# Loading the first pair of a batched matrix product in half-height pieces

## The chip, the cores and the metric

The kernel runs on one core of a Trainium2 chip. The metric is the device time of one execution in microseconds. TensorE (PE in the profile) multiplies matrices, VectorE (DVE) here converts float32 to bfloat16, ScalarE (ACT) copies results out of PSUM, SyncE (SP) issues all the transfers, and GpSimd (POOL) only waits at the end. The transfers themselves run on 16 DMA engines. On-chip memory (SBUF) has 128 partitions; a tile's first dimension is its partitions.

## What is computed

```
batch, m, k, n = 16, 512, 512, 512
a: (batch, k, m) float32     b: (batch, k, n) float32
out = matmul(a.transpose(0, 2, 1), b)      # (batch, m, n) float32
```

Each of the 16 batches is a 512x512x512 product in which both operands have k as their rows. 33.55 MB are read and 16.78 MB written.

## The kernel before

The 16 batches go in 8 pairs. One transfer brings both batches of a pair for one operand, 2 MB, into a tile `x` of 128 partitions: 64 partitions for each batch (`G = 2`, `Q = 64`), and in each partition 8 consecutive rows of k (`R = 8`), which is 16 KB in one run. So partition q of a batch holds k = 8q to 8q + 7. Four such tiles, x0 to x3, are used in turn: transfer n loads operand a for even n and b for odd n, of pair n // 2, into tile n % 4.

SyncE's program is written out by hand (lines 65 to 71). It issues the 16 loads in order. The first four have no wait; from n = 4 on (line 67) it waits on `s_in`, which VectorE raises when it has read a tile for the last time (lines 84 to 88, a one-element memset named `done`). After the loads come the stores of the first seven pairs, each waiting on `s_out` (line 70), all on the same queue. The last store is issued at line 133 after everything else.

VectorE (lines 73 to 88) converts each tile in two halves of 4 rows per partition (`V = 2`, `RV = 4`): first half v = 0 of a and b, then v = 1 of a and b. The wait on the loads stands at line 81, once per tile; the conversion is line 82. The v = 0 conversions of the next pair wait until TensorE has read the v = 0 buffers (`s_v`, line 76), those of v = 1 until the pair's products are finished (`s_mm`, line 78).

TensorE runs a loop of 8 pairs (line 92). For each it does 64 products of 64 rows of k by 128 by 512, 32 for each v, and the two batches of a pair use the upper and lower 64 rows of its array in turn (line 103). A sum over k is spread over v, r and 64 partitions; the order in which k is laid out doesn't matter so long as a and b have the same. ScalarE copies the sums to one of seven output tiles `o` (line 121) and signals the store (line 126).

## Time and profile before

| what | value |
|---|---|
| median of 3 runs | 124.03 us (123.98 to 124.14) |
| profiled execution: its own time | 123.82 us |
| profiled execution: span | 121.9 us |
| bytes moved | 50.33 MB, 413 GB/s over the span |
| DMA engines busy | 97.6% |
| PE / DVE / ACT busy | 51% / 31% / 26% |
| transfers | 8 of a, 8 of b, 8 of out, 2048 KB each |

The span is the time from the first to the last instruction in one profiled execution; the execution's own time is 1.9 us more. In the profile "L68" is line 68 of the kernel, an arrow "x<-in_a_dram" means that tile x is written from in_a_dram, "xN" counts instructions, and "A <- B" in a list of waits means that A waited for B (total us, times, longest). "SPq" is SyncE's own program. The DMA share is the mean busy share of the 16 DMA engines.

### The profile page before, as it was taken

The page shows a single profiled execution, that of the slowest core. Times are in us where ns is not written, and L with a number is a line of the kernel's source. Part 1 is how long each engine was busy: PE and PEld are TensorE (multiplying, and loading weights), DVE is VectorE, ACT ScalarE, POOL GpSimd, SP SyncE. Part 2 cuts the span into 40 slices and gives each one's busy share as a digit, 9 for nine tenths or more (in the row PEclk, how much of TensorE's full clock was granted, in tenths as well). Part 3 has the DMA queues.
Part 4 walks back from the last instruction along what each step waited for, and adds up shares of the span by engine and source line. Part 5 has one row for each costly group of instructions (what it writes and reads, how often), then busy time and mean ns, then how long its engine had stood idle before and what let it go on. Part 6 is the DMA issues. An engine that isn't in the chain of part 4 may idle for free. (4 is left out here: it accounts for less than half of the span.)

```text
span 121.9 us, 1261 instructions
## 1 busy us (share of the span) xinstructions
PE 62.5 (51%) x512; PEld 35.8 (29%) x512; DVE 38.0 (31%) x48; ACT 31.8 (26%) x41; POOL 0.2 (0%) x4
## 2 busy tenths in 40 slices
PE   0000099989669749969919988946960000000000
PEld 0000044546246314536605645624630000000000
DVE  0003560784194092474356247419000000000000
ACT  4000000480920830190470075091083000000000
POOL 0000000000000000000000000000000000000000
PEclk9999999999999977999995899999999655555555
DMA  5899999999999999999999999999999999999994
GB/s 108 360 430 430 436 430 430 430 430 430 430 430 430 430 430 436 430 430 430 430 430 430 430 430 430 436 390 428 428 430 430 430 428 430 430 430 428 428 428 175
DMA packets 4480, 50.33 MB, mean 413 GB/s; under 512 B 384, under 2 KB 384, under 8 KB 384
## 3 DMA queue, kind: packets, MB, share of 16 engines
q1 hardware_dynamic: 4480, 50.33, 97.6%
HBM read 33.55 MB, written 16.78 MB: 413 GB/s over the span
## 5 line engine op out<-in xcount | busy, mean ns | idle before, releaser
L103 PE MATMUL ps<-bbf,abf 64*128 64x512 bf16 x512 | 62.5, 403 | 27.9 <-PEq L98 27.9
L103 PEld LDWEIGHTS ps<-bbf,abf 64*128 64x128 bf16 x512 | 35.8, 114 | 54.1 <-issue 37.8
L121 ACT COPY o<-ps 128x1024 f32<-128x1024 f32 x32 | 30.1, 1026 | 59.8 <-PE ps L103 59.8
L82 DVE CAST abf<-x 128x2048 bf16<-128x2048 f32 x16 | 19.6, 1224 | 26.6 <-PE ps L103 17.6
L82 DVE CAST bbf<-x 128x2048 bf16<-128x2048 f32 x16 | 19.6, 1225 | 20.8 <-DMA x<-in_b_dram 20.8
L126 ACT ACTIVATE done<-done 1x1 uint32<-1x1 uint32 x8 | 1.6, 196 | 0.0
L121 ACT ACT_TABLE_LOAD x1 | 1.3, 1283 | 0.9 <-SPq L64 0.9
L88 DVE MEMSET done<- 1x1 f32 x16 | 0.9, 59 | 0.0
L148 POOL MEMSET const-bfloat16-1.0<- 128x1 bf16 x1 | 0.1, 101 | 0.0
L148 POOL MEMSET const-uint8-127<- 128x1 uint8 x1 | 0.1, 101 | 0.0
L148 POOL MEMSET const-float32-0.0<- 128x1 f32 x1 | 0.1, 98 | 0.2 <-issue 0.2
L148 POOL MEMSET const-float32-1.0<- 128x1 f32 x1 | 0.1, 98 | 0.0
## 6 DMA issues: line engine op xcount, KB each, us to landing
x<-in_a_dram SPq DMA_DIRECT2D x8, 2048.0 KB, 12.1
x<-in_b_dram SPq DMA_DIRECT2D x8, 2048.0 KB, 15.9
out_dram<-o SPq DMA_DIRECT2D x8, 2048.0 KB, 30.8
```

The source lines that it names most:

```text
L82: nc.vector.tensor_copy(out=(bbf_ts if n % 2 else abf_ts)[v][:], in_=x_ts[n % NX][:, v * RV:(v + 1) * RV, :],).then_inc(s_cast, 1)
L88: nc.vector.memset(dve_done[:, n:n + 1], 0.0).then_inc(s_in, 1)
L103: mm = nc.tensor.matmul(ps_ts[g][h][:, t % 2, :], a_m[:, t], bbf_ts[v][rows, r, :], start=(v == 0 and r == 0), stop=(v == V - 1 and r == R ...
L121: ev = nc.scalar.copy(out=o_ts[i % NO][:, g, 2 * h:2 * h + 2, :], in_=ps_ts[g][h][:])
L126: nc.scalar.memzero(act_done[:, i:i + 1]).then_inc(s_out, 1)
L148: nc = _bacc.Bacc("TRN2", target_bir_lowering=False, num_devices=1)
```

## The change

Only the first pair's two loads are touched. Each of them, one transfer of 128 partitions by 16 KB, becomes four transfers of 64 partitions by 8 KB, 512 KB each. The four are: half v = 0 of k for the first batch (partitions 0 to 63), the same for the second batch (partitions 64 to 127), and then both for v = 1. Within a piece, partition q holds k = 256 v + 4q to 256 v + 4q + 3, so the 64 runs of 8 KB of a piece lie side by side in DRAM, and the order of k over partitions differs from that of the other pairs, in a and b alike. All four pieces of an operand raise the same semaphore, and VectorE's wait on it at that place goes from 16 to 64 for the first use, and is higher by the same 48 in later uses of tiles x0 and x1. SyncE issues eight pieces, a's four and then b's four, ahead of the unchanged transfers of the second pair.

```diff
     in_v = [x.rearrange("(pair g) (q r) m -> pair (g q) r m", g=G, r=R) for x in (a, b)]
+
+    in0_v = [
+        x[0:G].rearrange("g (v q r) m -> v g q r m", v=V, r=RV) for x in (a, b)
+    ]
...
             if n >= NX:
                 nc.sync.wait_ge(s_in, n - NX + 1)
-            nc.sync.dma_start(x_ts[n % NX][:], in_v[n % 2][n // 2]).then_inc(s_x[n % NX], 16)
+            if n < 2:
+                for v in range(V):
+                    for g in range(G):
+                        nc.sync.dma_start(
+                            x_ts[n][g * Q:(g + 1) * Q, v * RV:(v + 1) * RV, :], in0_v[n][v, g]
+                        ).then_inc(s_x[n], 16)
+            else:
+                nc.sync.dma_start(x_ts[n % NX][:], in_v[n % 2][n // 2]).then_inc(s_x[n % NX], 16)
...
                     if v == 0:
-                        nc.vector.wait_ge(s_x[n % NX], 16 * (n // NX + 1))
+                        nc.vector.wait_ge(s_x[n % NX], 16 * (n // NX + 1 + (V * G - 1) * (n % NX < 2)))
```

## The prediction

> **What bounds the kernel now.** I read the page's slices and its queue summary first, because no compute engine is busy for more than 51% of the span (PE), so something else must set the time.

> ```profile
> DMA  5899999999999999999999999999999999999994
> GB/s 108 360 430 430 436 430 430 430 430 430 430 430 430 430 430 436 430 430 430 430 430 430 430 430 430 436 390 428 428 430 430 430 428 430 430 430 428 428 428 175
> ...
> q1 hardware_dynamic: 4480, 50.33, 97.6%
> ```

> The 16 DMA engines are busy for 97.6% of the span, in every slice from the third to the last but one, at a steady 428 to 436 GB/s (one dip to 390 where loads give way to stores). 50.33 MB at 0.429 MB per us is 117.3 us of the 121.9. So the kernel is one unbroken stream of transfers with a short start and tail, and only the stream's rate or a hole in it can move the end. The chain of waits that ended last doesn't show this: it runs from 83 to 93 us and its shares add up to under 8%, since the last store lies behind 28 us of other stores.

> Next the windows of the start, where the change lies. After the window and its length come busy us (and instructions) of PE, PEld, DVE, ACT and POOL, then clock, DMA share and GB/s.

> ```profile
> 1.00:2.00 1.00, 0.00 (x0) 0.00 (x0) 0.00 (x0) 1.00 (x1) 0.00 (x0) 1.00 0.24 66
> 2.00:4.00 2.00, 0.00 (x0) 0.00 (x0) 0.00 (x0) 0.18 (x1) 0.00 (x0) 1.00 0.94 229
> 4.00:8.00 4.00, 0.00 (x0) 0.00 (x0) 0.00 (x0) 0.00 (x0) 0.00 (x0) 1.00 0.99 426
> 8.00:12.50 4.50, 0.00 (x0) 0.00 (x0) 1.23 (x1) 0.00 (x0) 0.00 (x0) 1.00 1.01 433
> 120.00:121.80 1.80, 0.00 (x0) 0.00 (x0) 0.00 (x0) 0.00 (x0) 0.00 (x0) 0.50 0.07 27
> ```

> The engines are busy for 0.24 us of the second microsecond, so data starts at about 1.76 us. Bytes moved by 12.5 us: 0.066 + 2 x 0.229 + 4 x 0.426 + 4.5 x 0.433 = 4.18 MB, that is, the 4.194 MB of the first pair are through at 12.5 us. The ramp up to 4.0 us moves 0.52 MB where the steady rate would have moved 0.429 x 2.24 = 0.96 MB: it loses 1.0 us.

> Last the list of waits and the timeline with SyncE's issues, to see how much the stream is ahead of its issuer (start, us, then the instruction).

> ```profile
> DVE bbf L82 <- DMA x<-in_b_dram: 20.8, 8, 3.6
> DVE abf L82 <- DMA x<-in_a_dram: 8.8, 1, 8.8
> ...
> SPq L68 <- DVE done L88: 59.1, 12, 13.0
> ...
> 0.94 0.39 SPq L68 DMA_DIRECT2D x<-in_a_dram  x1
> 1.39 0.42 SPq L68 DMA_DIRECT2D x<-in_b_dram  x1
> 1.86 0.42 SPq L68 DMA_DIRECT2D x<-in_a_dram  x1
> 2.32 0.69 SPq L68 DMA_DIRECT2D x<-in_b_dram  x1
> 16.08 0.33 SPq L68 DMA_DIRECT2D x<-in_a_dram  x1
> ...
> 23.44 1.23 DVE L82 CAST bbf<-x 128x2048 bf16<-128x2048 f32 x1 [0.87 <-DMA x<-in_b_dram]
> ```

> VectorE waits for data in all eight pairs. The refill of the first buffer is issued at 16.08 us, while VectorE sees the fourth transfer land at 23.4 us: the queue is 7.3 us ahead.

> [...] The trace of before has only full-height transfers[...].
> [...] Here 24 DMAs run end to end at a DMA share of 1.0[...].

> **The change, part by part.**
> (1) Issue. Two issues become eight. At the pitch seen (1.39 - 0.94 = 0.45 us) the eighth begins at 0.94 + 7 x 0.45 = 4.1 us and the fourth full transfer ends its issue near 5.7 us instead of 3.0. Each piece of 0.524 MB takes 1.22 us even at full rate, so the queue never runs empty behind an issue every 0.45 us. What is queued behind on SyncE is the wait for the refill at 16 us or later. Cost 0; were the cover gone, 6 x 0.45 = 2.7 us.
> (2) Semaphores. The page has 384 packets under 512 B, which is 24 DMAs x 16 engines: each DMA uses all 16 and posts one small packet on each. Six more DMAs add 6 small packets per engine, where 24 leave no visible gap. Cost under 0.1 us.
> (3) Packet size. The runs go from 16 KB to 8 KB. The stores of before already move 8 KB runs, at 428 to 430 GB/s, like the loads. Cost 0.
> (4) Partitions. Each piece is 64 partitions high, and the four of an operand alternate: lower, upper, lower, upper half. All 16 engines take 4 rows each of the lower half, then 4 each of the upper half, in queue order. [...] The rate would be half: 8 x 26.8 = 214.5 GB/s. First pair: 4.194 / 0.2145 = 19.55 us instead of 4.194 / 0.429 = 9.78. The ramp nearly vanishes in it: between 2 and 4 us the old kernel already moved 229 GB/s, more than the new limit; I allow 0.25 us for the wait for the first bytes. The first pair is then through at 1.76 + 0.25 + 19.55 = 21.6 us, against 12.5: +9.1 us. [...] I take 9.0.
> (5) Waits. VectorE still waits for all of an operand (64 instead of 16), so nothing starts early on a piece; the other order of k is the same in a and b and costs nothing. The first cast of a moves from 8.8 to about 13, that of b from 13.7 to about 22.7.
> (6) Where the stall goes. It is a hole in the stream, and everything behind moves as one block: the refill issue and the end of the fourth transfer both move by 9, so the 7.3 us of lead stay. The last store's issue moves from 92.7 to about 102, while seven stores (14.7 MB, 34 us) keep the queue busy from about 91 to 125; it stays hidden with 23 us to spare. Nothing absorbs the hole, as no later part of the stream has spare rate.
> Sum: +9.0 us. The profiled execution's own time was 123.82 us (span 121.9, so 1.9 around it); it becomes 132.8 and the span 130.9. The median of before is 0.2 above its profiled run, so 124.03 + 9.0 = 133.0 us.

> **The rivals.**
> A. *[...] same or a bit faster.* Place: the first 12.5 us. [...] (1) to (3) cost nothing, and the first packet of each engine is half as long, so up to half of the ramp's 1.0 us may come back: 123.5 to 124.2 us. For it: no row of this trace shows a half-height transfer. [...] It decides if the first pair moves at over about 424 GB/s, where the loss is within 0.1 us; every 5 GB/s below costs another 0.1 us.
> B. *The engines fall out of step; part of the loss.* [...] A piece is 4 packets of 8 KB, 0.31 us each at full rate. [...] For it: the ramp shows that the engines don't start alike. Against: the end is set by the slowest engine[...].
> C. *Worse than half.* [...] Against: the trace's gapless queue. 135 to 145 us.

> **How the numbers follow.** The forecast ([...] 131.5 to 134.5) has 0.66, B (126 to 131.5) 0.18, A 0.12, C 0.04. The time is 133.0. The range 129.0 to 134.5 holds the forecast's range and rather more than half of B, near 0.78 to 0.8. This kernel's runs can tell about 0.2% (0.25 us) from no change. Faster by more than that lies only in A, a quarter of it: 0.03. Same is the rest of A: 0.09. Slower: 0.88.

> **What would show it.** In the windows the new kernel should move about 215 GB/s from 2 to 21 us with the DMA share still near 1.0 (each packet just takes twice as long), then 429 again. First cast of a near 13 us, of b near 22.7, refill issue near 25, lead still about 7 us; last store's issue near 102; stores and later loads unchanged. Eight issues of 512 KB about 0.45 us apart. The prediction is wrong if the early windows stay near 429 GB/s (A), lie between 260 and 350 (B), if the DMA share falls well below 1 there (C), or if the later loads catch up part of the delay.

## The result

The changed kernel takes 132.67 us, median of 6 runs (132.38 to 132.95), against 124.09 us for the kernel before in the same runs (123.98 to 124.30): a ratio of 1.0692, with a 95% interval of 1.0674 to 1.0709. That is 8.6 us slower; 133.0 had been forecast. The profiled execution of the new kernel took 132.68 us with a span of 130.7 us.

First the page of the changed kernel: the slices of the span (3.27 us each here) and the queue summary.

```profile
DMA  3999999999999999999999999999999999999994
GB/s 90 223 221 216 223 206 266 426 456 421 446 416 421 461 401 426 456 421 446 416 421 461 401 426 456 421 446 389 439 429 416 436 431 416 436 431 416 436 434 201
...
q1 hardware_dynamic: 4832, 50.33, 98.0%
```

The bytes are the same and the engines are as busy as before, but five slices near the start run at 206 to 223 GB/s. From the eighth on the stream is what it was. The DMA row alone would have hidden this: a 9 there says that the engines are occupied, not that they move much.

The windows of the changed kernel show the slow stretch more closely (columns as in the prediction; the last two are DMA share and GB/s). A packet is what one engine moves at a time, in these loads one run of 8 or 16 KB. A window counts every packet whole if it begins there: that is why shares come out above 1.00 and why the GB/s of neighbouring windows scatter.

```profile
2.00:4.00 2.00, 0.00 (x0) 0.00 (x0) 0.00 (x0) 0.18 (x1) 0.00 (x0) 1.00 0.90 221
4.00:8.00 4.00, 0.00 (x0) 0.00 (x0) 0.00 (x0) 0.00 (x0) 0.00 (x0) 1.00 1.05 227
8.00:12.00 4.00, 0.00 (x0) 0.00 (x0) 0.00 (x0) 0.00 (x0) 0.00 (x0) 1.00 1.02 215
12.00:16.00 4.00, 0.00 (x0) 0.00 (x0) 1.23 (x1) 0.00 (x0) 0.00 (x0) 1.00 0.99 213
16.00:20.00 4.00, 0.00 (x0) 0.00 (x0) 0.00 (x0) 0.00 (x0) 0.00 (x0) 1.00 1.06 227
20.00:21.00 1.00, 0.00 (x0) 0.00 (x0) 0.00 (x0) 0.00 (x0) 0.00 (x0) 1.00 1.08 221
21.00:24.00 3.00, 0.00 (x0) 0.00 (x0) 1.37 (x2) 0.00 (x0) 0.00 (x0) 1.00 0.98 350
```

The sum up to 21.0 us is 2 x 0.221 + 4 x (0.227 + 0.215 + 0.213 + 0.227) + 0.221 = 4.19 MB: the last packets of the first pair begin at 21.0 us instead of 12.5. For the rate, windows of 2.4 us are better, because they lie behind the start and each holds the bytes of one piece:

```profile
4.40:6.80 2.40, 0.00 (x0) 0.00 (x0) 0.00 (x0) 0.00 (x0) 0.00 (x0) 1.00 1.01 218
...
14.00:16.40 2.40, 0.00 (x0) 0.00 (x0) 0.26 (x1) 0.00 (x0) 0.00 (x0) 1.00 1.02 218
```

The three windows between these two have 218 GB/s too.

Last the timeline of the changed kernel, VectorE and SyncE, to see how the rest moved:

```profile
13.03 1.23 DVE L93 CAST abf<-x 128x2048 bf16<-128x2048 f32 x1 [13.03 <-DMA x<-in_a_dram]
22.63 1.23 DVE L93 CAST bbf<-x 128x2048 bf16<-128x2048 f32 x1 [8.38 <-DMA x<-in_b_dram]
...
32.17 1.23 DVE L93 CAST bbf<-x 128x2048 bf16<-128x2048 f32 x1 [0.47 <-DMA x<-in_b_dram]
...
0.95 2.46 SPq L75 DMA_DIRECT2D x<-in_a_dram  x4
3.46 2.52 SPq L75 DMA_DIRECT2D x<-in_b_dram  x4
6.01 0.59 SPq L79 DMA_DIRECT2D x<-in_a_dram  x1
6.64 0.43 SPq L79 DMA_DIRECT2D x<-in_b_dram  x1
25.05 0.33 SPq L79 DMA_DIRECT2D x<-in_a_dram  x1
...
101.31 0.70 SPq L144 DMA_DIRECT2D out_dram<-o  x1
```

The first refill is issued at 25.05 us (16.08 before) and b of the second pair is used at 32.17 (23.44), so the queue's lead is 7.1 us (7.4 before). The last store is issued at 101.31 us (92.71). Everything behind the first pair moved by 8.6 to 9.0 us, nearly as a block; these are single executions, and no later part took back more than 0.4 us.

### The profile page after: what moved, and what is told of

Its sections match the earlier page's. It is cut to its first block, busy times and chain, and to the rows that moved or that the text cites. A ratio compares the mean times of both kernels' runs of the same rounds, so it can differ in the third digit from the quotient of the medians.

```text
span 130.7 us, 1267 instructions
## 1 busy us (share of the span) xinstructions
PE 61.2 (47%) x512; PEld 36.3 (28%) x512; DVE 38.0 (29%) x48; ACT 31.8 (24%) x41; POOL 0.2 (0%) x4
## 2 busy tenths in 40 slices
DMA packets 4832, 50.33 MB, mean 385 GB/s; under 512 B 480, under 2 KB 480, under 8 KB 480
## 3 DMA queue, kind: packets, MB, share of 16 engines
q1 hardware_dynamic: 4832, 50.33, 98.0%
## 5 line engine op out<-in xcount | busy, mean ns | idle before, releaser
L114 PE MATMUL ps<-bbf,abf 64*128 64x512 bf16 x512 | 61.2, 397 | 37.8 <-PEq L109 37.8
L114 PEld LDWEIGHTS ps<-bbf,abf 64*128 64x128 bf16 x512 | 36.3, 113 | 62.3 <-issue 45.9
```

The source lines that it names most:

```text
L114: mm = nc.tensor.matmul(ps_ts[g][h][:, t % 2, :], a_m[:, t], bbf_ts[v][rows, r, :], start=(v == 0 and r == 0), stop=(v == V - 1 and r == R ...
```

## The experiments

The theory: a piece that lies wholly in partitions 0 to 63, or wholly in 64 to 127, moves at half rate, because of where it lands. The rivals: it is the number or size of the pieces, the shorter runs, reading a block of DRAM that lies side by side, or any height under 128. Except where said, every kernel is the changed one with only the loads of the first pair cut in another way, and with VectorE's first wait set to the number of pieces. The edits are shown shortened: calls stand on one line, and the `then_inc` of the semaphore and the changed wait are left out.

**Full height, two pieces (128 partitions by 8 KB).**

```diff
-                    for g in range(G):
-                        nc.sync.dma_start(x_ts[n][g * Q:(g + 1) * Q, v * RV:(v + 1) * RV, :], in0_v[n][v, g])
+                    rr = slice(v * RV, (v + 1) * RV)
+                    nc.sync.dma_start(x_ts[n][:, rr, :], in_v[n][0][:, rr, :])
```

> The first pair in two pieces per operand by half of k, each of all 128 partitions by 8 KB (1 MB). Theory [...] 124.1 us, with 429 GB/s in the first 12 us; a little less, to 123.7, if the start of the stream gains from shorter first packets. Rival (runs of 8 KB instead of 16 KB are slow to read): near 132.7 us. Rival (each extra transfer costs a fixed time; six extra cost 8.6): two extra cost 2.9, so 127.0.

Measured 124.34 us, ratio to the kernel before 1.0018 (1.0004 to 1.0033). The windows of this run:

```profile
4.00:8.00 4.00, 0.00 (x0) 0.00 (x0) 0.00 (x0) 0.00 (x0) 0.00 (x0) 1.00 1.01 424
8.00:12.00 4.00, 0.00 (x0) 0.00 (x0) 1.23 (x1) 0.00 (x0) 0.00 (x0) 1.00 1.01 428
```

The same 8 KB runs into full height move at full rate, so the length of the runs isn't the cause. The 0.27 us that this kernel is slower arise later: in the packets' records its first pair ends at 12.98 us, that of the kernel before at 13.11, but its dip where loads give way to stores is deeper (see the last experiment).

**Full height, four pieces (128 partitions by 4 KB).** The same cut, into four.

> As many pieces of the same 512 KB as in the change, four per operand, but each of 128 partitions by 4 KB. Theory [...]: 124.1 us, down to 123.6 if shorter first packets help the start. Rival (the number or the size of the transfers): 132.7 us. Rival (short runs): 132.7 us or more.

Measured 124.69 us, ratio 1.0054 (1.0037 to 1.0071). As many pieces of the same 512 KB as in the change lose 0.6 us, not 8.6. The loss can be seen: in this run's windows the stream moves 362 GB/s from 4 to 8 us and 385 from 8 to 12.

```profile
4.00:8.00 4.00, 0.00 (x0) 0.00 (x0) 0.00 (x0) 0.00 (x0) 0.00 (x0) 1.00 0.99 362
8.00:12.00 4.00, 0.00 (x0) 0.00 (x0) 1.23 (x1) 0.00 (x0) 0.00 (x0) 1.00 1.00 385
```

These pieces read runs of 4 KB that lie 16 KB apart in DRAM. The run "The same reads, spread over 128 partitions", further down, moves as many packets of the same size (5344 in all in both) from blocks that lie side by side, and its windows have 391 and 423 GB/s. So the small packets alone don't cost this; the runs that lie apart remain as a possible cause, which no run here shows alone.

**Half height alone (64 partitions by 16 KB, two pieces).** Long runs and the old order of k.

```diff
-                for v in range(V):
-                    for g in range(G):
-                        nc.sync.dma_start(x_ts[n][g * Q:(g + 1) * Q, v * RV:(v + 1) * RV, :], in0_v[n][v, g])
+                for g in range(G):
+                    pp = slice(g * Q, (g + 1) * Q)
+                    nc.sync.dma_start(x_ts[n][pp], in_v[n][0][pp])
```

> Only the height: two pieces per operand, one per batch, 64 partitions by 16 KB (1 MB), rows and order of k as in the kernel before. Theory [...]: the full loss, 132.7 us within 0.7, about 220 GB/s up to 21 us. Rival (number of transfers): two extra, 127.0 us. Rival (8 KB runs or the new order of k): 124.1 us. [...]

Measured 133.19 us, ratio 1.0738 (1.0718 to 1.0758). The windows of this run:

```profile
4.00:8.00 4.00, 0.00 (x0) 0.00 (x0) 0.00 (x0) 0.00 (x0) 0.00 (x0) 1.00 0.94 197
8.00:12.00 4.00, 0.00 (x0) 0.00 (x0) 0.00 (x0) 0.00 (x0) 0.00 (x0) 1.00 1.00 205
12.00:16.00 4.00, 0.00 (x0) 0.00 (x0) 1.23 (x1) 0.00 (x0) 0.00 (x0) 1.00 1.13 238
16.00:20.00 4.00, 0.00 (x0) 0.00 (x0) 0.00 (x0) 0.00 (x0) 0.00 (x0) 1.00 1.01 213
```

The height alone brings the whole loss, and neither the number of pieces nor the run length nor the order of k is needed for it.

It is even 0.5 us more than in the change, and the traces' records of single packets show where that lies. At full height a packet of 16 KB takes 611 ns and one of 8 KB 309. Sorted by their start, the packets of the slow pieces come in rounds of sixteen, as many as there are engines. In this run's third piece the first round after the crossing from one half to the other takes 1146 ns for a packet (median), the next 1263, then 1294 and 1295, where twice 611 is 1222. So packets within one half take up to 6% more than double, and each crossing gives some time back. The change has pieces of half the size and crosses twice as often: its rounds of 8 KB take 593, 561, 627 and 645 ns, 607 on average, where twice 309 is 618. Over the whole pair the two patterns differ by 0.6 us. Why a crossing helps is open. If engines out of step were the reason, the last packets before a crossing should be short as well, and those take 1281 ns or more.

**The same height elsewhere (partitions 32 to 95 in one piece).** This separates "fewer than 128 partitions" from "one half of the partitions". The edit is against the run before this one.

```diff
-                for g in range(G):
-                    pp = slice(g * Q, (g + 1) * Q)
+                for pp in (slice(32, 96), slice(0, 32), slice(96, 128)):
                     nc.sync.dma_start(x_ts[n][pp], in_v[n][0][pp])
```

> The same runs of 16 KB, cut elsewhere: per operand one piece of partitions 32 to 95 (64 high, 1 MB), then 0 to 31 and 96 to 127 (0.5 MB each). Theory [...]: the piece 32 to 95 [...] costs nothing although it is 64 high; only the other half of the bytes goes at 220 GB/s: 2.1 MB at 0.220 instead of 0.429 is 4.6 us, so 128.4 us within 0.7. Rival (any piece of fewer than 128 partitions is slow): 132.7 us or more. Rival (number of transfers, four extra): 129.8 us, which the windows tell apart: [...] full speed and half speed alternate within each operand.

Measured 128.72 us, ratio 1.0367 (1.0342 to 1.0392): a loss of 4.65 us where 4.6 had been reckoned, half of the 9.1 us of the run before. The windows of this run:

```profile
4.00:6.00 2.00, 0.00 (x0) 0.00 (x0) 0.00 (x0) 0.00 (x0) 0.00 (x0) 1.00 1.06 393
6.00:8.00 2.00, 0.00 (x0) 0.00 (x0) 0.00 (x0) 0.00 (x0) 0.00 (x0) 1.00 1.09 238
8.00:10.00 2.00, 0.00 (x0) 0.00 (x0) 0.00 (x0) 0.00 (x0) 0.00 (x0) 1.00 0.96 205
10.00:12.00 2.00, 0.00 (x0) 0.00 (x0) 0.58 (x1) 0.00 (x0) 0.00 (x0) 1.00 0.94 336
12.00:14.00 2.00, 0.00 (x0) 0.00 (x0) 0.64 (x1) 0.00 (x0) 0.00 (x0) 1.00 1.06 320
14.00:16.00 2.00, 0.00 (x0) 0.00 (x0) 0.00 (x0) 0.00 (x0) 0.00 (x0) 1.00 0.95 213
```

The piece of 32 to 95 is first in each operand, and in its time the rate is high (393; for b between 10 and 14 us, mixed with its neighbours, 320 to 336). In the time of 0 to 31 and 96 to 127 it falls to 205 to 238. The first piece of the run before had the same size and the same place in the queue, and was slow. So a piece 64 partitions high is not slow in itself: it is slow when all of it lies on one side of partition 64.

**The same reads, spread over 128 partitions.** The change's eight blocks of DRAM, in its order.

```diff
-        x[0:G].rearrange("g (v q r) m -> v g q r m", v=V, r=RV) for x in (a, b)
+        x[0:G].rearrange("g (v p r) m -> v g p r m", v=V, r=2) for x in (a, b)
...
-                            x_ts[n][g * Q:(g + 1) * Q, v * RV:(v + 1) * RV, :], in0_v[n][v, g]
+                            x_ts[n][:, 2 * w:2 * w + 2, :], in0_v[n][v, g]      # w = v * G + g
```

> The change's eight reads, each the same contiguous 512 KB of DRAM in the same order, but spread over 128 partitions by 4 KB each. This puts the two batches' rows on the wrong partitions, so the first pair's products are not the reference's; the bytes and all instructions are. Theory [...]: 124.1 us. Rival (sixteen engines reading one 512 KB block side by side in DRAM are slow): 132.7 us.

Measured 124.82 us, ratio 1.0048 (1.0023 to 1.0073). Its twelve times spread from 123.86 to 125.94, more than those of any other kernel here, so its 0.6 us is a rough figure. It is far from 132.7: the reading side is not the cause.

```profile
2.00:4.00 2.00, 0.00 (x0) 0.00 (x0) 0.00 (x0) 0.18 (x1) 0.00 (x0) 1.00 0.95 330
4.00:8.00 4.00, 0.00 (x0) 0.00 (x0) 0.00 (x0) 0.00 (x0) 0.00 (x0) 1.00 1.01 391
8.00:12.00 4.00, 0.00 (x0) 0.00 (x0) 1.23 (x1) 0.00 (x0) 0.00 (x0) 1.00 1.03 423
```

From 1 to 12 us this run moved 357 GB/s on average, and the kernel before 360. What it lost in its profiled execution lies later, in two slices of 395 and 374 GB/s where loads give way to stores (390 in the kernel before).

**Lower halves from SyncE, upper halves from ScalarE.**

```diff
-                        nc.sync.dma_start(
+                        (nc.scalar if g else nc.sync).dma_start(
```

> The change's eight pieces, but the four of the lower half are issued by SyncE and the four of the upper half by ScalarE, so that each engine has both halves in two queues at the same time. If the engines alternate packets and fall out of step[...]: 124 to 126 us. [...] the loss stays: about 132 us. My guess is between, 129 us, nearer to the full loss. If the second queue only shifted the issue, the windows would show 220 GB/s as before.

Measured 131.17 us, ratio 1.0562 (1.0533 to 1.0591). The queue summary of its page shows that the second queue was used, and its windows what came of it:

```profile
q1 hardware_dynamic: 4512, 48.24, 91.1%
q10 hardware_dynamic: 320, 2.10, 6.9%
...
4.00:8.00 4.00, 0.00 (x0) 0.00 (x0) 0.00 (x0) 0.72 (x1) 0.00 (x0) 1.00 1.02 221
8.00:12.00 4.00, 0.00 (x0) 0.00 (x0) 0.00 (x0) 0.00 (x0) 0.00 (x0) 1.00 0.99 240
12.00:16.00 4.00, 0.00 (x0) 0.00 (x0) 1.23 (x1) 0.00 (x0) 0.00 (x0) 1.00 1.04 254
```

(The summary's figures are packets, MB and share.) The rate rises from 221 to 240 and 254 GB/s, and 1.5 of the 8.6 us come back. That is 8% of the first pair's 19 us. Although both halves are on offer, the engines still do nearly the same half at the same time. The packets' records, which name the queue, show it: sorted by their start, of every sixteen packets 11 to 16 come from the same queue. At first the engines take whole pieces in turn from the two queues; from 8.4 us on they change queue every packet or two, but most of them together.

**The second pair too.** `if n < 2` becomes `if n < NX`, with the same views for pair 1.

> The change made in the second pair too (tiles x2 and x3), 16 half-height pieces. Theory (each half-height byte takes twice as long and nothing later gives time back): the loss doubles, 8.6 + 8.6 to 9.5 us, so 141.3 to 142.2 us. If the lead of the queue over the refill absorbed some: less. If the loss were tied to the start of the stream: 132.7 us.

Measured 142.03 us, ratio 1.1440 (1.1420 to 1.1461). The loss is 17.97 us; the second pair adds 142.03 - 132.67 = 9.4 us. So it isn't tied to the start, and the lead absorbs none of it. The second pair lies behind the slow start, so its loss is the plain difference of the rates: 4.194 MB at 218 GB/s take 19.2 us and at 429 GB/s 9.8. The slices of this run (3.5 us each) stay between 208 and 225 GB/s for ten of them:

```profile
GB/s 119 208 225 208 225 220 225 211 213 220 218 269 435 449 430 412 444 435 449 398 440 435 449 402 435 435 449 412 419 419 440 416 440 416 433 428 421 440 419 213
```

**The last store in two halves**, in the kernel before, to see the other direction:

```diff
-    nc.sync.dma_start(out_v[pairs - 1], o_ts[(pairs - 1) % NO][:])
+    for pp in (slice(0, 64), slice(64, 128)):
+        nc.sync.dma_start(out_v[pairs - 1][pp], o_ts[(pairs - 1) % NO][pp])
```

> The kernel before with its last store alone cut into two half-height ones of 1 MB (partitions 0 to 63, 64 to 127). [...] 2.1 MB at 0.220 instead of 0.429 MB per us is +4.6 us, 128.7 us. If the limit is one of writing to SBUF only: 124.1 us.

Measured 126.54 us, ratio 1.0197 (1.0178 to 1.0215): +2.5 us. Its control cuts the same store by batch, at full height:

> The last store cut in two as in the run with half-height stores, but by batch instead of by partition: two of 1 MB, 128 partitions each. If the 2.5 us lost there came from the height: 124.1 us here. If it came from cutting the last store at all: 126.5 us.

Measured 123.91 us, ratio 0.9997 (0.9986 to 1.0007): no loss. So the half height costs in stores too, but half of the 4.6 us expected. The end of the run with half-height stores, by windows:

```profile
114.00:116.00 2.00, 0.00 (x0) 0.00 (x0) 0.00 (x0) 0.00 (x0) 0.00 (x0) 0.50 0.99 418
116.00:118.00 2.00, 0.00 (x0) 0.00 (x0) 0.00 (x0) 0.00 (x0) 0.00 (x0) 0.50 1.13 336
118.00:122.00 4.00, 0.00 (x0) 0.00 (x0) 0.00 (x0) 0.00 (x0) 0.00 (x0) 0.50 0.96 233
122.00:124.00 2.00, 0.00 (x0) 0.00 (x0) 0.00 (x0) 0.00 (x0) 0.00 (x0) 0.50 0.20 66
```

From 116 us on these windows hold 0.672 + 0.932 + 0.132 = 1.74 MB, so 0.36 MB of the 2.10 had already gone at full rate, and 2 us more ran at 336 before the rate fell to 233. Engines that are still busy with the store before would do this, but the trace speaks against it for the start: the last of the 16 small packets that end that store begins before 115.8 us, and the packets begun from 116 to 117 us still move 418 GB/s. Why a store loses less than a load stays open.

**Two attempts to beat the kernel before.** The full-height run in two pieces had shown slices of 363 and 374 GB/s where loads give way to stores (390 in the kernel before). So the first store was put ahead of the last pair's two loads (and left out of the later loop), alone and together with the two-piece loads:

```diff
         for n in range(2 * pairs):
+            if n == 2 * pairs - 2:
+                nc.sync.wait_ge(s_out, 1)
+                nc.sync.dma_start(out_v[0], o_ts[0][:]).then_inc(s_o0, 16)
```

> The kernel before with the first store issued ahead of the last pair's two loads, to see whether the dip where loads give way to stores (390 GB/s in one slice of before, about 0.1 us) can be filled. If the dip comes from the queue running short of loads there: 123.9 us. If every change from loads to stores has it: 124.1 us or a little more.

> The first pair in two full-height pieces per operand and the first store issued ahead of the last pair's loads. The pieces had gained about 0.15 us at the start and lost 0.6 us in a deeper dip between loads and stores. If the early store fills that dip: 123.8 us, a little below both kernels. If the dip stays: 124.3 us.

Measured 124.19 us, ratio 1.0013 (1.0000 to 1.0027), and 124.34 us, ratio 1.0035 (1.0021 to 1.0050). Neither is faster, and the second is 0.4 us slower. In the second, the slices show the dip moved forward (363 and 392) and not filled, with a second small one behind it (408):

```profile
GB/s 83 398 430 427 446 438 427 438 438 427 427 432 427 438 427 432 432 427 432 432 427 427 363 392 451 432 427 427 408 427 427 427 427 430 427 427 427 427 432 107
```

## Why the prediction was right, step by step

The bound: shown. One stream of transfers sets the time, and a loss of 8.5 us in the first pair appears as 8.6 us at the end; two pairs lose twice as much.

Steps 1 and 2, issue and semaphores: right in costing nothing, wrong in a size. Eight issues took 2.46 + 2.52 us, 0.62 each and not 0.45, and the issue of the second pair's b ended at 7.1 us, not 5.7. A piece takes 2.4 us to move at the slow rate (and 1.22 at full rate), so it stayed hidden, as said.

Step 3, packet size: right for 8 KB within what can be measured (0.27 us with two full-height pieces). The four pieces of 4 KB, which the change doesn't use, cost 0.6 us. That is also all that six more transfers of 512 KB at full height cost together, so no larger fixed cost per transfer shows.

Step 4, partitions: this carries the result. That a half-height piece moves at half rate was the author's estimate, without a line of the trace behind it. The runs now show the loss, in the form of which half of the partitions is reached (in the run with the piece 32 to 95, 393 GB/s in that piece's time and 205 to 238 in that of the others). What holds the rate down within one half is not shown. The rate was put at 214.5 GB/s, half of the full one: 429 / 16 is 26.8 for each engine, and 8 times that was taken. Measured were 218, so 4.19 MB take 19.2 us and not 19.55. That it came so close is partly luck: packets later within a half took longer than double (627 and 645 ns, where twice 309 is 618), and those just after a crossing gave a little more than that back (593 and 561). The first packet begins at 2.29 us and not at 2.01, so the first pair ends where it was reckoned (at 21.66 us in the packets' records, for 21.6). The 12.5 us of the kernel before, and the 1.76 us for its first data, were read too early, from windows that count a packet where it begins: its first packet begins at 1.96 us and its first pair ends at 13.1. So the loss was 8.5 us and not 9.1.

Steps 5 and 6: the casts came at 13.03 and 22.63 us (forecast 13 and 22.7), the refill at 25.05 (25), the lead 7.1 us (7.3; the lines of before give 7.4), the last store's issue at 101.3 (102).

Rival A, no loss: excluded by the early windows (213 to 227 GB/s, not over 424). Rival B, engines out of step: no sign of it in the change (218 GB/s, not 260 to 350, and 645 ns for the packets before a crossing), and only in part with two queues (221 to 254 GB/s). Rival C, worse than half: not in the sum, though packets within one half took up to 6% more than double (1295 ns, where twice 611 is 1222).

## What to carry to other kernels

## What was not expected

Half-height stores lose too, but 2.5 us for 2.1 MB where loads lose about 4.3 (8.6 for 4.19 MB). Issuing the two halves from two engines brings back only 1.5 of 8.6 us. With pieces of 64 partitions by 16 KB three packets of four took more than twice the full-height time (1263 to 1295 ns, where twice 611 is 1222), and the first ones after a crossing less (1146). And the issue of a half-height load took SyncE longer, 0.62 us, than a full-height one four times its size before (0.45 us from one to the next).
